# A pair of up projections: both sums of one matrix ahead of the other's, and the second raw sum placed behind a split

## The chip, the cores and the metric

The kernel runs on one core of one Trainium2 chip. The metric is the device time of one execution in microseconds (us). Each kernel is run several times, and the median is what is compared.

## The reference

The program is a trunk of two layers (`DEPTH = 2`) over 512 rows of width 1024, all in float32. Each layer has two half steps with a SwiGLU of inner width 2816, one ahead of a mixer of three head groups and one behind it:

```python
def swiglu(x, w1, w3, w2):
    return (jax.nn.silu(x @ w1) * (x @ w3)) @ w2

for l in range(DEPTH):
    h = x + 0.5 * swiglu(rms_norm(x, ffn1_norm[l]), ffn1_w1[l], ffn1_w3[l], ffn1_w2[l])
    ...
    h = h + y @ w_out[l]
    h = h + 0.5 * swiglu(rms_norm(h, ffn2_norm[l]), ffn2_w1[l], ffn2_w3[l], ffn2_w2[l])
    x = rms_norm(h, final_norm[l])
```

The change touches only `x @ w1` and `x @ w3`, the up projections, of the four half steps. `y` is the mixer's output: a causal convolution, sliding window attention and attention to 256 memory tokens, side by side.

## The kernel before

**Operands in two parts.** A float32 operand is split into a high part and a small rest. ScalarE copies it into the high part (`whi`), VectorE subtracts that from the operand and gets the rest (`wlo`); both instructions are in `split` (lines 147 to 149). A product is then high by high, rest by high and high by rest.

**Chunks and pairs.** The 2816 inner columns are 22 chunks of 128. In each half step chunks 0 to 3 are computed plainly (`up`, `gate`), and the others in pairs f, f + 1 by `up_pair` (line 362): f = 4 in a branch of its own (the plain pair, `PLAIN`), and f = 6, 8 ... 20 in the `else` branch. These are 8 pairs in each of 4 half steps, 32 in all, and the change is in that branch only. The down projection (`begin`, line 546) follows by quarters of the inner width, (first chunk, chunks) = (0, 6), (6, 6), (12, 6), (18, 4). Two chunks of the next quarter are computed ahead of each quarter's down projection, so pairs come in groups: f = 4, 6, then 8, 10, 12, then 14, 16, 18, then 20, with a stretch of down projection behind each group.

**Seven products.** For each matrix i (0 is w1, 1 is w3) a pair is a 2 by 2 block product, done with seven half-size products in place of eight, in the manner of Strassen and Winograd. The left operands are sums of blocks of the normed input, M1 to M7. They are made once for each half step by the class `Seven`, on VectorE and ScalarE, partly while the first pairs run. The right operands are sums of blocks of the weights, each 128 x 1024 words, and each of these units is split once (`unit`, line 357). A pair has seven units:

- raw0 and raw1, the weights of the two matrices as loaded (line 105): product 1 and product 2
- sum0 and sum1, made in place over raw0 and raw1 by two adds each (lines 443 and 444, the raw adds): product 6 and product 3
- X0 and X1 (`wsum`), the sum of two chunks, made by a load that SP issues (line 369) and a second one that GpSimd's queue adds on top (line 370): product 7 and product 5
- z, one half of the next chunk for both matrices (line 374): product 4, for each matrix

The units came in the order raw0, raw1, sum0, sum1, X0, X1, z: three loops over i and a last unit. The first raw add of a matrix reads X of the same matrix, so it has to wait for X to land.

**Products in PSUM.** Products 1, 6 and 5 of a matrix accumulate into one bank `x[i]` (tag `pt`) by `product`, 12 matmuls of 256 columns on line 381. Each time ScalarE copies the running sum to `part` before the next product goes on (lines 438, 449 and 458). Products 2, 3, 7 and 4 go into banks of their own (`po`, `cf`, `mm`) by `beside`, four matmuls of 512 columns and four of 256 on line 389. VectorE adds the pieces up (`add`, lines 399 and 400, and `summed`, line 402) into `u` and `g`. Behind these come `silu` (line 467), the multiplication and the split of the gated result (lines 468 to 472), which the down projection reads.

**Buffers.** There are 3 buffers for the raw tiles (raw0, raw1, z and the weights of the down projection take turns), 3 for `wsum`, and 4 each for `whi` and `wlo`. A load can start when the last reader of what the buffer held is done, which for a weight tile is VectorE's subtract or a raw add. SP issues its loads one after the other, and so does GpSimd.

**The order.** The order on each engine is set by a scheduler, which takes the source as its starting point and places instructions when a model has them ready. `tc.issue_after(x)` makes it place the enclosed instructions behind x only; `queued()` uses it to keep matmuls behind the last ones. While the mixer's weights and the memory tokens are prepared (`memory`, line 678) in the first layer, small instructions of that work lie between those of the pairs: `rsq` (line 195), a power on GpSimd, is one of them.

Of the kernel before, what the change touches and what calls it, by code (L numbers as in the profile page):

```python
# [65 lines left out]
def trunk(ctx: ExitStack, tc: tile.TileContext, xT, memT, pos, w1a, w3a, w2a, w1b, w3b, w2b,  # L66
          wconv, wqk, wvm, wmem, wout, gains, small, rows, consts, out):
    nc = tc.nc
    V, G, A, T = nc.vector, nc.gpsimd, nc.scalar, nc.tensor
# [21 lines left out]
    def bank(shape, tag):  # L91

        if tag == "mm":
            return ps_mm.tile(shape, F32, tag=tag, name=tag)
        return ps_ax.tile(shape, F32, tag=tag, name=tag, bufs=1 if tag == "cf" else 2)

    def tm(name, tag="t", bufs=None):
        return tmp.tile([P, S], F32, tag=tag, name=name, **({"bufs": bufs} if bufs else {}))
# [4 lines left out]
    def raw_tile(src, cols):  # L103
        raw = wst.tile([P, UNIT], F32, tag="raw", name="raw", bufs=3)
        nc.sync.dma_start(raw[:, 0:cols], src)
        return raw
# [40 lines left out]
    def split(hi, lo, x, on):  # L147
        a = A.activation(hi, x, AF.Copy)  # L148
        return a, on.tensor_tensor(out=lo, in0=x, in1=hi.bitcast(F32), op=ALU.subtract)  # L149
# [12 lines left out]
    def pair():  # L162
        return (wst.tile([P, UNIT], F32R, tag="whi", name="whi"), wst.tile([P, UNIT], F32R, tag="wlo", name="wlo"))
# [23 lines left out]
    def blk(k, n=P):  # L187
        return slice(k * n, (k + 1) * n)
# [97 lines left out]
    QW = 512  # L286
# [66 lines left out]
    def gated():  # L353
        p = gated_pair()
        return [at(p, ALL, i, ALL) for i in range(2)]

    def unit(x):
        p = pair()
        split(p[0], p[1], x, V)
        return p  # L360

    def up_pair(l, w13, f, M):

        raw = [raw_tile(w13[i][l, f], D) for i in range(2)]
        X = []
        for i in range(2):

            x = wst.tile([P, UNIT], F32, tag="aux", name="wsum", bufs=3)
            nc.sync.dma_start(x.rearrange("p (f c) -> p f c", f=2), w13[i][l, f : f + 2, :, 0:QW].rearrange("f p c -> p f c"))
            G.dma_start(x, w13[i][l, f + 1], accum_op=ALU.add)  # L370
            X.append(x)
        z = wst.tile([P, UNIT], F32, tag="raw", name="raw", bufs=3)
        for i in range(2):
            nc.sync.dma_start(z[:, blk(i, QW)], w13[i][l, f + 1, :, QW:])
        x0, x1 = blk(0, QT), blk(1, QT)

        def product(ps, w, half, j, first=False):


            for n, (part, q) in enumerate([(0, q) for k in range(4) for q in ((k, 0), (k, 1))] + [(1, (k, 0)) for k in range(4)]):  # L380
                tail[0] = T.matmul(ps, w[part][:, blk(4 * half + q[0])], M.m[j][q[0]][:, q[1]], skip_group_check=True,  # L381
                                   start=first and not n, stop=n == 11)

        def beside(ps, w, half, j, first=False):


            def go(out, part, n):
                for k in range(4):
                    tail[0] = T.matmul(out, w[part][:, blk(4 * half + k)], M.m[j][k][:, 0:n], skip_group_check=True,  # L389
                                       start=first and not part and k == 0, stop=part == 1 and k == 3)  # L390

            go(ps, 0, 2)
            go(ps[:, 0], 1, 1)

        u, g = (tmp.tile([P, 2, S], F32, tag=t, name=t, bufs=n) for t, n in (("u", 1), ("g", 2)))
        part = [tm("part", "sq", 2) for _ in range(2)]
        to = (u, g)

        def add(out, a, b):
            V.tensor_tensor(out=out, in0=a, in1=b, op=ALU.add)  # L400

        def summed(out, ps, a):
            add(out, ps[:, 0], a)
            add(out, out, ps[:, 1])

        if f == PLAIN:
            xy = [bank([P, S], "po") for _ in range(2)]
            zv = [bank([P, S], "pt") for _ in range(2)]
            for i in range(2):
                w = unit(raw[i])  # L410
                product(xy[i][:, x0], w, 0, 1, first=True)
                product(xy[i][:, x1], w, 1, 2)
                A.activation(part[i], xy[i], AF.Copy)
                add(to[i][:, 0, x0], part[i][:, x0], part[i][:, x1])

                add(raw[i][:, 0:QW], raw[i][:, 0:QW], X[i][:, QW:])
                add(raw[i][:, QW:], raw[i][:, QW:], raw[i][:, 0:QW])
            for i in range(2):
                w = unit(raw[i])
                product(xy[i][:, x0], w, 0, 6)  # L420
                A.activation(part[i][:, x1], xy[i][:, x0], AF.Copy)
                product(zv[i][:, x0], w, 1, 3, first=True)
            for i in range(2):
                w = unit(X[i])
                product(xy[i][:, x0], w, 1, 5)
                A.activation(part[i][:, x0], xy[i][:, x0], AF.Copy)
                product(zv[i][:, x1], w, 0, 7)
                add(to[i][:, :, x1], zv[i].rearrange("p (n t) -> p n t", n=2), part[i][:, x0].unsqueeze(1).to_broadcast([P, 2, QT]))
            w = unit(z)
            for i in range(2):  # L430
                product(zv[i][:, x1], w, i, 4)
                add(to[i][:, 1, x0], zv[i][:, x1], part[i][:, x1])
        else:
            x = [bank([P, QT], "pt") for _ in range(2)]
            for i in range(2):
                w = unit(raw[i])
                product(x[i], w, 0, 1, first=True)
                A.activation(part[i][:, x0], x[i], AF.Copy)
                y = bank([P, 2, QT], "po")
                beside(y, w, 1, 2, first=True)  # L440
                summed(to[i][:, 0, x0], y, part[i][:, x0])

                add(raw[i][:, 0:QW], raw[i][:, 0:QW], X[i][:, QW:])
                add(raw[i][:, QW:], raw[i][:, QW:], raw[i][:, 0:QW])
            c, v = [bank([P, 2, QT], t) for t in ("cf", "mm")], []
            for i in range(2):
                w = unit(raw[i])
                product(x[i], w, 0, 6)
                A.activation(part[i][:, x1], x[i], AF.Copy)
                beside(c[i], w, 1, 3, first=True)  # L450
            for i in range(2):
                w = unit(X[i])
                v.append(bank([P, 2, QT], "po"))
                beside(v[i], w, 0, 7, first=True)
                A.activation(to[i][:, 1, x1], v[i][:, 0], AF.Copy)
                add(to[i][:, 1, x1], to[i][:, 1, x1], v[i][:, 1])
                product(x[i], w, 1, 5)
                A.activation(part[i][:, x0], x[i], AF.Copy)
                summed(to[i][:, 0, x1], c[i], part[i][:, x0])
                add(to[i][:, 1, x1], to[i][:, 1, x1], part[i][:, x0])  # L460
            w = unit(z)
            for i in range(2):
                beside(v[i], w, i, 4)
                summed(to[i][:, 1, x0], v[i], part[i][:, x1])
        out = gated()
        for n, sign in enumerate((1.0, -1.0)):
            A.activation(u[:, n], u[:, n], AF.Silu, scale=sign)
        M.gated = V.tensor_tensor(out=g, in0=g, in1=u, op=ALU.mult)
        for n, sign in enumerate((1.0, -1.0)):
            hi, lo = out[n]  # L470
            A.activation(hi, g[:, n], AF.Copy, scale=sign)
            V.scalar_tensor_tensor(out=lo, in0=g[:, n], scalar=sign, in1=hi.bitcast(F32), op0=ALU.mult, op1=ALU.subtract)  # L472
        return out

    def ffn(l, w13, w2, x, sums, factors, last, at_product, aside=None, closing=None):
# [60 lines left out]
        for q, (f0, nf) in enumerate(QUARTERS):  # L536
            ahead = 2 if q + 1 < len(QUARTERS) else 0
            for f in range(f0, f0 + nf + ahead, 2):
                if f not in g:
                    g[f], g[f + 1] = up_pair(l, w13, f, M)  # L540
                    if f == PLAIN:
                        with tc.issue_after(M.gated.ins):
                            rescale = after()
# [614 lines left out]
    for l in range(L):  # L1158
        x, new = nxt.x, Stat("st")
# [163 lines left out]
```

## Time and profile before

| | |
|---|---|
| median of 3 runs | 1759.15 us |
| lowest and highest | 1758.93 and 1760.65 us |
| the profiled execution, its time | 1760.35 us |
| its span in the profile | 1758.5 us |
| TensorE instructions | 10004 |
| bytes moved by DMA | 253.49 MB |

The span runs from the first to the last instruction of the profiled execution; 1.85 us of that execution lie around it. PE is TensorE (PEld its weight loads), DVE is VectorE, ACT ScalarE, POOL GpSimd and SPq the queue that issues most loads. A row of the view in order of time has the start (us from the span's start), the duration, the engine, the line, and output <- inputs; the brackets at its end give the idle time ahead of it and what ended that. A row of the view by stretches has the stretch, its length, and the busy time of each engine in it, with the number of instructions. A row of the DMA table has the queue, the count, the size of each transfer and the median time from issue to landing.

### The profile page before, as it was taken

The page shows a single profiled execution, that of the slowest core. Times are in us where ns is not written, and L with a number is a line of the kernel's source. Part 1 is how long each engine was busy: PE and PEld are TensorE (multiplying, and loading weights), DVE is VectorE, ACT ScalarE, POOL GpSimd, SP SyncE. Part 2 cuts the span into 40 slices and gives each one's busy share as a digit, 9 for nine tenths or more (in the row PEclk, how much of TensorE's full clock was granted, in tenths as well). Part 3 has the DMA queues.
Part 4 walks back from the last instruction along what each step waited for, and adds up shares of the span by engine and source line. Part 5 has one row for each costly group of instructions (what it writes and reads, how often), then busy time and mean ns, then how long its engine had stood idle before and what let it go on. Part 6 is the DMA issues. An engine that isn't in the chain of part 4 may idle for free.

```text
span 1758.5 us, 26405 instructions
## 1 busy us (share of the span) xinstructions
PE 1742.3 (99%) x10004; PEld 1524.0 (87%) x10004; DVE 1370.0 (78%) x2218; ACT 907.7 (52%) x1437; POOL 196.0 (11%) x220
## 2 busy tenths in 40 slices
PE   9999999999999999999999999999999999999997
PEld 7889889888888989898889898988888889898986
DVE  7969878689877868686778787776898768686866
ACT  6546445356765535353656354544567655453533
POOL 1001000006121000000010010000251210000000
PEclk9999999999999999999999999999999999999999
DMA  9456646257247546565566465542671666464632
GB/s 286 112 167 169 179 121 161 73 159 164 86 93 183 142 134 163 143 161 146 150 149 162 150 168 156 158 142 71 162 165 54 136 152 181 131 168 133 153 99 84
DMA packets 96335, 253.49 MB, mean 144 GB/s; under 512 B 9808, under 2 KB 16208, under 8 KB 96208
## 3 DMA queue, kind: packets, MB, share of 16 engines
q1 hardware_dynamic: 77200, 190.45, 34.8%
q0 software_dynamic: 19008, 61.35, 19.5%
q8 instruction: 79, 1.29, 0.3%
q14 instruction: 48, 0.39, 0.1%
HBM read 249.67 MB, written 2.10 MB: 143 GB/s over the span
## 4 chain that ended last, share of the span: by engine, by line
PE 92%; DVE 4%; DMA 2%; issue 1%; ACT 0%; SPq 0%; DVEq 0%; POOLq 0%; ACTq 0%
PE pt L381 16%; PE mm L180 14%; PE mm L182 14%; PE mm L181 14%; PE po L389 13%; PE po L381 2%; PE mm L389 2%; PE cf L389 2%; PE po L180 2%; PE po L182 2%; PE po L181 2%; PE po L928 2%; DMA wsum<-in_w3a 1%; PE mm L876 1%; PE cf L182 1%
## 5 line engine op out<-in xcount | busy, mean ns | idle before, releaser
L148 ACT ACTIVATE whi<-raw 128x1024 fp32r<-128x1024 f32 (+3 forms) x346 | 326.3, 947 | 429.1 <-PE mm L181 202.7
L149 DVE TENSOR_TENSOR wlo<-raw,whi 128x1024 fp32r<-128x1024 f32 (+3 forms) x346 | 374.7, 1088 | 99.4 <-ACT whi L148 98.2
L181 PE MATMUL mm<-glo,whi 128*128 128x512 f32 (+1 forms) x752 | 292.2, 389 | 0.0
L180 PE MATMUL mm<-ghi,whi 128*128 128x512 f32 (+1 forms) x752 | 292.0, 390 | 0.0
L182 PE MATMUL mm<-ghi,wlo 128*128 128x512 f32 (+1 forms) x734 | 285.3, 389 | 0.0
L564 DVE SCALAR_TENSOR_TENSOR h<-mm,h 128x512 f32<-128x512 f32 x126 | 86.3, 688 | 112.2 <-PE mm L182 111.8
L180 PEld LDWEIGHTS mm<-ghi,whi 128*128 128x128 f32 x752 | 141.2, 188 | 29.2 <-DVE h L564 1.2
L181 PEld LDWEIGHTS mm<-glo,whi 128*128 128x128 f32 x752 | 141.3, 188 | 28.4 <-DVE glo L472 0.2
L182 PEld LDWEIGHTS mm<-ghi,wlo 128*128 128x128 f32 x734 | 137.9, 188 | 27.7
L389 PE MATMUL po<-xlo,whi 128*128 128x512 f32 x512 | 139.5, 394 | 0.9 <-DVE g L400 0.9
L1058 DVE SCALAR_TENSOR_TENSOR there<-ypad,par,there 128x512 f32<-128x512 f32 x180 | 136.0, 779 | 1.3
L389 PEld LDWEIGHTS po<-xlo,whi 128*128 128x128 f32 x512 | 89.6, 189 | 15.2 <-DVE g L400 1.8
L180 PE MATMUL mm<-xhi,whi 128*128 128x512 f32 x256 | 101.6, 398 | 0.0
L182 PE MATMUL mm<-xhi,wlo 128*128 128x512 f32 x256 | 99.9, 390 | 0.0
L181 PE MATMUL mm<-xlo,whi 128*128 128x512 f32 x256 | 99.6, 389 | 0.0
L149 DVE TENSOR_TENSOR wlo<-wsum,whi 128x1024 fp32r<-128x1024 f32 x72 | 87.5, 1215 | 0.3 <-ACT whi L148 0.3
L389 PEld LDWEIGHTS po<-xlo,wlo 128*128 128x128 f32 x512 | 78.3, 188 | 10.6
L148 ACT ACTIVATE whi<-wsum 128x1024 fp32r<-128x1024 f32 x72 | 76.2, 1058 | 19.2 <-PE po L389 15.9
L381 PE MATMUL pt<-xhi,whi 128*128 128x256 f32 x576 | 81.9, 283 | 0.0
L389 PE MATMUL po<-xlo,wlo 128*128 128x256 f32 x512 | 81.2, 280 | 0.0
L381 PEld LDWEIGHTS pt<-xhi,whi 128*128 128x128 f32 x576 | 74.8, 190 | 0.5
L381 PE MATMUL pt<-ml,whi 128*128 128x256 f32 x512 | 72.9, 282 | 0.0
(397 smaller groups left out, 3605.7 us busy)
## 6 DMA issues: line engine op xcount, KB each, us to landing
raw<-in_w2a SPq DMA_DIRECT2D x48, 384.0 KB, 3.8
raw<-in_w2b SPq DMA_DIRECT2D x48, 384.0 KB, 3.7
raw<-in_w1a SPq DMA_DIRECT2D x26, 512.0 KB, 3.5
raw<-in_w3a SPq DMA_DIRECT2D x26, 512.0 KB, 3.7
raw<-in_w1b SPq DMA_DIRECT2D x26, 512.0 KB, 3.5
raw<-in_w3b SPq DMA_DIRECT2D x26, 512.0 KB, 3.6
wsum<-in_w1a SPq DMA_DIRECT2D x18, 512.0 KB, 4.5
wsum<-in_w3a SPq DMA_DIRECT2D x18, 512.0 KB, 3.6
```

What stands on the lines that cost most here:

```text
L148: a = A.activation(hi, x, AF.Copy)
L149: return a, on.tensor_tensor(out=lo, in0=x, in1=hi.bitcast(F32), op=ALU.subtract)
L180: T.matmul(ps, a[0], b[0], start=first, stop=False, **more)
L181: T.matmul(ps, a[0], b[1], start=False, stop=False, **more)
L182: tail[0] = T.matmul(ps, a[1], b[0], start=False, stop=last, **more)
L381: tail[0] = T.matmul(ps, w[part][:, blk(4 * half + q[0])], M.m[j][q[0]][:, q[1]], skip_group_check=True, start=first and not n, stop=n == 11)
L389: tail[0] = T.matmul(out, w[part][:, blk(4 * half + k)], M.m[j][k][:, 0:n], skip_group_check=True, start=first and not part and k == 0, st ...
L564: added = V.scalar_tensor_tensor(out=h[:, d, :], in0=ps, scalar=0.5, in1=h[:, d, :], op0=ALU.mult, op1=ALU.add)
L876: tail[0] = T.matmul(pp[i][:, z, :], q, k, start=not masked, stop=True, skip_group_check=True)
L928: tail[0] = T.matmul(po[:, 2 * c + i, :], ptb[:, i, j, :], v, start=(j == 0), stop=(j == nk - 1))
L1058: V.scalar_tensor_tensor(out=cv[:, c, :], in0=ypad[:, c, j : j + S], scalar=conv_w[:, c, j : j + 1], in1=cv[:, c, :], op0=ALU.mult, op1=AL ...
```

## The change

The raw adds leave the first loop and go into the second, each pair of them directly ahead of the split of its sum. The first of the two may only be placed behind the subtract of the unit that was split last (`unit.at`): for matrix 0 that is raw1's, for matrix 1 it is X0's. The second and third loops become one, so the order of the units is now raw0, raw1, sum0, X0, sum1, X1, z. No computation is added or left out.

```diff
     def unit(x):
         p = pair()
-        split(p[0], p[1], x, V)
+        unit.at = split(p[0], p[1], x, V)[1]
         return p
...
                 y = bank([P, 2, QT], "po")
                 beside(y, w, 1, 2, first=True)
                 summed(to[i][:, 0, x0], y, part[i][:, x0])
-
-                add(raw[i][:, 0:QW], raw[i][:, 0:QW], X[i][:, QW:])
-                add(raw[i][:, QW:], raw[i][:, QW:], raw[i][:, 0:QW])
             c, v = [bank([P, 2, QT], t) for t in ("cf", "mm")], []
             for i in range(2):
+                with tc.issue_after(unit.at.ins):
+                    add(raw[i][:, 0:QW], raw[i][:, 0:QW], X[i][:, QW:])
+                add(raw[i][:, QW:], raw[i][:, QW:], raw[i][:, 0:QW])
                 w = unit(raw[i])
                 product(x[i], w, 0, 6)
                 A.activation(part[i][:, x1], x[i], AF.Copy)
                 beside(c[i], w, 1, 3, first=True)
-            for i in range(2):
                 w = unit(X[i])
                 v.append(bank([P, 2, QT], "po"))
                 beside(v[i], w, 0, 7, first=True)
```

Three places show how the programs differ. The first is VectorE in a steady pair, f = 16 of the first half step. `raw_2531` and `raw_2533` are raw0 and raw1 (later sum0 and sum1), `wsum_2535` and `wsum_2538` are X0 and X1, and L149 is the subtract of a split. Before:

```order
L149 TENSOR_TENSOR wlo_2551<-raw_2531,whi_2550 128x1024
L400 TENSOR_TENSOR u_2318<-u_2318,po_2440 128x256
L400 TENSOR_TENSOR raw_2531<-raw_2531,wsum_2535 128x512
L400 TENSOR_TENSOR raw_2531<-raw_2531 128x512
L149 TENSOR_TENSOR wlo_2581<-raw_2533,whi_2580 128x1024
L400 TENSOR_TENSOR u_2318<-cf_2384,part_2320 128x256
L400 TENSOR_TENSOR u_2318<-u_2318,part_2320 128x256
L400 TENSOR_TENSOR g_2319<-g_2319,po_2471 128x256
L400 TENSOR_TENSOR raw_2533<-raw_2533,wsum_2538 128x512
L400 TENSOR_TENSOR u_2318<-u_2318,cf_2384 128x256
L149 TENSOR_TENSOR wlo_2613<-raw_2531,whi_2612 128x1024
```

In the changed program the same stretch begins with raw1's split:

```order
L149 TENSOR_TENSOR wlo_2579<-raw_2533,whi_2578 128x1024
L400 TENSOR_TENSOR raw_2531<-raw_2531,wsum_2535 128x512
L400 TENSOR_TENSOR g_2319<-g_2319,po_2471 128x256
L400 TENSOR_TENSOR raw_2531<-raw_2531 128x512
L400 TENSOR_TENSOR u_2318<-po_2413,part_2320 128x256
L400 TENSOR_TENSOR g_2319<-mm_2381,part_2321 128x256
L400 TENSOR_TENSOR g_2319<-g_2319,part_2321 128x256
L400 TENSOR_TENSOR u_2318<-u_2318,po_2413 128x256
L400 TENSOR_TENSOR g_2319<-g_2319,mm_2381 128x256
L149 TENSOR_TENSOR wlo_2611<-raw_2531,whi_2610 128x1024
L400 TENSOR_TENSOR g_2319<-po_2471,part_2321 128x256
L149 TENSOR_TENSOR wlo_2636<-wsum_2535,whi_2635 128x1024
```

The raw adds of matrix 0 moved from ahead of raw1's split to behind it. Those of matrix 1, which stood ahead of sum0's split, are gone from this stretch and stand behind X0's split, its last row.

The second place is the two queues that load X1 (`wsum_1652`) for f = 10 of the first half step, which is a pair during whose time the memory tokens are prepared. This is the difference on SP's queue:

```order
 L105 DMA raw_1645<-in_w1a 128x1024
+L369 DMA wsum_1652<-in_w3a 128x2x512
 L105 DMA raw_1647<-in_w3a 128x1024
-L369 DMA wsum_1652<-in_w3a 128x2x512
 L369 DMA wsum_1875<-in_w1a 128x2x512
```

And this is the difference on GpSimd's queue, where `rsq` is of `memory`:

```order
 L197 TENSOR_TENSOR rsq4_1395<-hv4_1392,nhalf_113 128x4
+L370 DMA wsum_1652<-in_w3a 128x1024
 L197 TENSOR_TENSOR rsq4_1411<-hv4_1408,nhalf_113 128x4
-L370 DMA wsum_1652<-in_w3a 128x1024
 L370 DMA wsum_1875<-in_w1a 128x1024
```

X1's load moved ahead of raw1's load (`raw_1647`), and its accumulate ahead of the second `rsq`.

The third place is TensorE in the pair f = 6 of the first half step. `pt_782` and `pt_783` are `x[0]` and `x[1]`; `mh`, `ml`, `xhi` and `xlo` hold M1 to M7, and x8 counts equal rows. On `pt_782` the rows that read `mh` are product 1, those that read `ml` product 6, those that read `xhi` product 5. Before:

```order
L381 MATMUL pt_782<-mh_344,whi_784 128x256 x8
L381 MATMUL pt_782<-mh_344,wlo_785 128x256 x4
L381 MATMUL pt_783<-mh_344,whi_814 128x256 x8
L381 MATMUL pt_783<-mh_344,wlo_815 128x256 x4
L389 MATMUL mm_845<-xhi_501,whi_871 128x512 x4
L381 MATMUL pt_782<-ml_345,whi_846 128x256 x8
L381 MATMUL pt_782<-ml_345,wlo_847 128x256 x4
L389 MATMUL mm_845<-xhi_501,wlo_872 128x256 x4
L381 MATMUL pt_783<-ml_345,whi_871 128x256 x8
L381 MATMUL pt_783<-ml_345,wlo_872 128x256 x4
L381 MATMUL pt_782<-xhi_501,whi_896 128x256 x8
L381 MATMUL pt_782<-xhi_501,wlo_897 128x256 x4
```

In the changed program:

```order
L381 MATMUL pt_782<-mh_344,whi_784 128x256 x8
L381 MATMUL pt_782<-mh_344,wlo_785 128x256 x4
L381 MATMUL pt_783<-mh_344,whi_812 128x256 x8
L381 MATMUL pt_783<-mh_344,wlo_813 128x256 x4
L381 MATMUL pt_782<-ml_345,whi_844 128x256 x8
L381 MATMUL pt_782<-ml_345,wlo_845 128x256 x4
L381 MATMUL pt_782<-xhi_501,whi_869 128x256 x8
L381 MATMUL pt_782<-xhi_501,wlo_870 128x256 x4
L389 MATMUL po_873<-xlo_502,whi_869 128x512 x4
L389 MATMUL po_873<-xlo_502,wlo_870 128x256 x4
L381 MATMUL pt_783<-ml_345,whi_902 128x256 x8
L389 MATMUL mm_841<-xhi_501,whi_902 128x512 x4
```

Product 5 of matrix 0 now follows product 6 of the same matrix directly, in the same bank; product 6 and the half of product 3 of matrix 1 that stood between them moved behind it.

## Prediction

> **What bounds the kernel.** I read the page first: the span, the engines' shares, the chain that ended last.
>
> ```profile
> span 1758.5 us, 26405 instructions
> PE 1742.3 (99%) x10004; PEld 1524.0 (87%) x10004; DVE 1370.0 (78%) x2218; ACT 907.7 (52%) x1437; POOL 196.0 (11%) x220
> PE 92%; DVE 4%; DMA 2%; issue 1%; ACT 0%; SPq 0%; DVEq 0%; POOLq 0%; ACTq 0%
> ```
>
> TensorE has work on record for all but 16.2 us of the span, and 92% of the chain is its own. An order of the same matmuls can only win back its idle time, so the next view asks how much of that lies in the up pairs: busy time by stretch. The first five stretches are the only ones around changed pairs in which the record shows TensorE idle; the other three stand for the rest.
>
> ```profile
> core 0: us, PE busy (x) PEld busy (x) DVE busy (x) ACT busy (x) POOL busy (x), PEclk, DMA share, GB/s
> 54.00:100.00 46.00, 44.79 (x319) 41.58 (x318) 40.88 (x60) 27.16 (x41) 3.45 (x4) 1.00 0.64 163
> 134.00:205.00 71.00, 70.32 (x454) 63.59 (x454) 65.27 (x144) 40.62 (x67) 9.62 (x9) 1.00 0.69 179
> 786.00:812.00 26.00, 25.45 (x149) 22.23 (x148) 21.48 (x37) 12.79 (x22) 1.72 (x2) 1.00 0.72 190
> 932.00:970.00 38.00, 37.45 (x266) 34.82 (x265) 31.33 (x47) 20.31 (x32) 3.45 (x4) 1.00 0.73 188
> 1009.00:1072.00 63.00, 62.10 (x419) 56.76 (x418) 54.41 (x93) 37.95 (x63) 7.67 (x8) 1.00 0.63 170
> 576.00:616.00 40.00, 40.00 (x302) 38.46 (x301) 35.00 (x49) 24.76 (x38) 3.45 (x4) 1.00 0.60 159
> 1446.00:1484.00 38.00, 38.00 (x290) 36.63 (x289) 34.75 (x48) 23.94 (x36) 3.47 (x4) 1.00 0.59 155
> 650.00:790.00 140.00, 140.00 (x882) 126.83 (x881) 106.50 (x166) 68.80 (x106) 8.66 (x10) 1.00 0.59 157
> ```
>
> Idle: 1.21, 0.68, 0.55, 0.55 and 0.90 us, together 3.89; elsewhere zero. A matmul's record outlasts its issue, so this is a little short. Rows of TensorE in order of time show by how much.
>
> ```profile
> 182.21 0.63 PE L389 MATMUL po<-xlo,wlo 128*128 128x256 f32 x4
> 183.47 1.19 PE L389 MATMUL cf<-xhi,whi 128*128 128x512 f32 x4 [0.63 <-ACT whi L148]
> 240.58 1.12 PE L381 MATMUL pt<-ml,whi 128*128 128x256 f32 x8
> 241.54 0.64 PE L381 MATMUL pt<-ml,wlo 128*128 128x256 f32 x4
> 242.02 1.09 PE L389 MATMUL cf<-xhi,whi 128*128 128x512 f32 x4
> 242.95 0.63 PE L389 MATMUL cf<-xhi,wlo 128*128 128x256 f32 x4
> 243.42 1.12 PE L381 MATMUL pt<-ml,whi 128*128 128x256 f32 x8
> ```
>
> By the starts, a `product` holds TensorE 1.44 us (240.58 to 242.02) and a `beside` 1.40 (to 243.42); four narrow matmuls take 0.47 (242.95 to 243.42). So the four at 182.21 were issued by 182.68, and the gap behind them cost 0.79 us where the record shows 0.63. Scaled by 0.79/0.63 the idle 3.89 is about **4.9 us, all that the order of the pairs can win**.
>
> **What the change moves.** It adds no instruction, matmul or byte; 2 adds and 2 splits per pair change places, in 32 pairs. The prices, from VectorE, ScalarE and the queues in order of time:
>
> ```profile
> 264.04 0.38 SPq L369 DMA_DIRECT2D wsum<-in_w3a  x1
> 268.16 0.86 POOL L370 DMA_DIRECT2D wsum<-in_w3a  x1 [20.27 <-DVE wlo L149]
> 275.48 0.69 DVE L400 TENSOR_TENSOR raw<-raw,wsum 128x512 f32<-128x512 f32 x1 [2.61 <-DMA wsum<-in_w3a]
> 276.09 0.41 DVE L400 TENSOR_TENSOR g<-mm,part 128x256 f32<-128x256 f32 x1
> 277.08 1.22 DVE L149 TENSOR_TENSOR wlo<-raw,whi 128x1024 fp32r<-128x1024 f32 x1
> 278.22 0.68 DVE L400 TENSOR_TENSOR raw<-raw 128x512 f32<-128x512 f32 x1
> ```
>
> By starts again: a raw add 0.61 us (275.48 to 276.09), a split 1.14 (277.08 to 278.22).
>
> *X1's sum comes earlier and is asked for later.* X1's buffer is the one that X0 of the pair before gives back. In this pair its load was issued at 264.04, the accumulate at 268.16, and VectorE stood 2.61 us for it at 275.48, with sum0's split of the same pair behind that add. Afterwards X0's split lies ahead of sum1's, so the buffer is free one split sooner, SP issues X1 ahead of raw1, and the add waits behind three more splits. I expect this wait to go. It wins nothing by itself: the last of the stretches above (650 to 790), which holds such pairs, has TensorE at 140.00 of 140. It is reserve.
>
> *Fewer adds ahead of raw1 and sum0* (second stretch and fifth). Here VectorE binds: 65.27 of 71 us. The gap at 183.47 waits for sum0. Before, its split had up to four raw adds of its pair ahead, now two: 2 x 0.61 = 1.2 us sooner, more than the 0.79 lost there. Both stretches lose 1.25 x (0.68 + 0.90) = 2.0 us. I take **-1.5**, not all of it, because of the next part; ends -2.0 and 0.
>
> *POOL, in the second stretch only.* The accumulate for X1 now stands ahead of the second `rsq` of `memory`, whose result VectorE multiplies in ahead of X1's split.
>
> ```profile
> 144.63 1.15 POOL L197 TENSOR_TENSOR rsq<-hv,nhalf 128x4 f32<-128x4 f32 x1 [8.61 <-DVE hv L643]
> 147.09 2.52 POOL L197 TENSOR_TENSOR rsq<-hv,nhalf 128x4 f32<-128x4 f32 x1 [1.31 <-DVE ypad L603]
> 169.21 0.38 SPq L369 DMA_DIRECT2D wsum<-in_w3a  x1
> 174.20 0.86 POOL L370 DMA_DIRECT2D wsum<-in_w3a  x1 [17.55 <-DMA wsum<-in_w3a]
> 149.20 1.21 DVE L149 TENSOR_TENSOR wlo<-wsum,whi 128x1024 fp32r<-128x1024 f32 x1
> 152.83 0.65 PE L381 MATMUL pt<-xhi,wlo 128*128 128x256 f32 x4
> ```
>
> From X0's split the path is load to accumulate (4.1 us at 264.04, 5.0 at 169.21), 0.9 for the issue, 1.15 to 2.52 for `rsq`: 6.2 to 8.4. VectorE has some 5.7 us of other work there by the order (a split, two raw adds, 3.3 us of small ones), so it would stand 0.5 to 2.7 us. X1's split was 2.4 us ahead of TensorE (150.41 to 152.83) and everything in front is up to 1.2 sooner, so I price it **0**, ends 0 and +1.5 (2.7 less 1.2). The Trainium skill, SBUF — State Buffer, section "SBUF: two separate sides", says that a GpSimd instruction is shut out of a shared port while VectorE works on two SBUF inputs, which are what the raw adds are. By that rule `rsq` takes the 2.52 and this term is its upper end; the two rows 1.15 and 2.52 agree with it, but nothing here isolates it.
>
> *The first pair behind the plain one* (first stretch and fourth; 1.25 x (1.21 + 0.55) = 2.2 us lost). raw1's split again comes sooner, but TensorE then reaches the last product of the plain pair, which needs M4, and M4's split keeps its place among Seven's sums. I take **-0.5**, nearer to nothing; ends -2.2 and 0. The third stretch loses 0.7 us behind one late add of a pair; I take **-0.3**, ends -0.7 and 0.
>
> *A new wait: product 6, copy, product 5.* Both go into `x[i]`, and the copy on ScalarE has to read the bank in between. Before, at least 1.4 us of other matmuls lay there by the order. Now the pair f = 6 of the first, second and fourth half step has product 5 directly behind product 6.
>
> ```profile
> 242.22 0.39 ACT L449 ACTIVATE part<-pt 128x256 f32<-128x256 f32 x1 [0.79 <-PE pt L381]
> ```
>
> That product's issue ended at 242.02, the copy at 242.61: 0.6 us, three times **+1.8**. Below, 0: TensorE would have stood there anyway. Above, +5.0: a copy of a weight tile ahead of it (1.06, as below) each time. Elsewhere one pair has 0.2 us of matmuls left between (f = 8 of the first half step), one 0.9, all others 1.9 to 5.6, which covers 0.6.
>
> **Sum.** -1.5 + 0 - 0.5 - 0.3 + 1.8 = -0.5 us. The profiled execution took 1760.35 us (span 1758.5 and 1.85 around it), which would become 1759.85; the median of the runs shown is 1.2 lower, so the forecast is 1759.15 - 0.5, about **1758.6**. Ends: -4.9 and +6.5.
>
> **Rivals.**
>
> *Slower: raw1 lands late.* Its buffer returns with sum1's split, which now stands behind X0's split and an add, and SP issues it behind X1.
>
> ```profile
> 258.61 0.33 SPq L105 DMA_DIRECT2D raw<-in_w3a  x1
> 268.62 1.06 ACT L148 ACTIVATE whi<-raw 128x1024 fp32r<-128x1024 f32 x1 [0.51 <-PE pt L381]
> raw<-in_w3a SPq DMA_DIRECT2D x26, 512.0 KB, 3.7
> ```
>
> Load issued 258.61, first read 268.62: 10.0 us, of which 3.7 is the median landing. Later by a split, an add and an issue (1.14 + 0.61 + 0.38), 7.9 remain. It decides once a load takes longer: ScalarE's queue stops, and the part copies behind it too. The accumulate above took 7.3 (268.16 to 275.48), so it is not absurd. Third pairs of a quarter are the thinnest; there are eight. At about 1 us each: +8, 1767. I give it, with the upper end of the copies, 0.17.
>
> *Faster: the starved stretches close and the copies hide.* All of -4.9: 1754.3. For it: VectorE's 2.61 us of waiting turn into reserve just where it binds. Against: M4 and the three copies. 0.13.
>
> *Faster: TensorE is not full at all.* In the last stretch its weight loads are busy 126.83 of 140 us. If a tenth of the open 13.2 came back over 36 pairs of 7 x 2.84 us (716 us), that is 6.7 us: 1752.4. Against: 1.44 and 1.40 us for a product and a beside hold wherever no wait is shown, and the change alters no shape. The Trainium skill, Perfetto Trace Analysis, section "Identifying the Most-Contended Engine", says that busy matmul time is a poor measure of what is left and weight-load time a good one; by that rule this would be the case. I give this rival 0.03.
>
> **How the numbers follow.** A measurement here tells about 0.2%, 3.5 us, from no change: faster is below 1755.6, slower above 1762.7. The forecast and all between these has 0.67, faster 0.13 + 0.03, slower 0.17. The range of 8 in 10 is 1754.5 to 1764.5: the ends of the sum are 1754.3 and 1765.7, and about a tenth is left out on each side, which is most of the two larger rivals.
>
> **What would show it.** Right: no wait of a raw add for X1's sum in steady pairs; TensorE idle in the second and fifth stretch well under 0.7 and 0.9 us; three new waits of TensorE on `part` L449 of about 0.5 at the f = 6 pairs. Wrong: VectorE standing on `rsq` for over 2.5 us near 151 us and TensorE after it; ScalarE waiting for `raw<-in_w3a`; more or less than 1.44 us per product; a total outside the range.

## The result, and the profile after

The changed kernel takes 1775.55 us (median of 4 runs, 1774.80 to 1779.11) beside 1759.04 us for the kernel before in the same comparison: 1.0096 times as long, 95% interval 1.0079 to 1.0114. That is 16.5 us slower, outside the range on record. Its profiled execution took 1779.11 us, 3.6 more than the median; readings of it explain that execution, and the experiments are compared by their medians.

The page of the changed kernel, with the same three rows as before:

```profile
span 1777.3 us, 26372 instructions
PE 1750.1 (98%) x10004; PEld 1527.2 (86%) x10004; DVE 1364.1 (77%) x2218; ACT 904.6 (51%) x1437; POOL 199.1 (11%) x220
PE 86%; DVE 7%; DMA 2%; ACT 2%; issue 2%; POOL 0%; SPq 0%; DVEq 0%; ACTq 0%
```

TensorE is idle for 27.2 us of the record (1777.3 less 1750.1), and was for 16.2. It is also 7.8 us longer busy with the same 10004 instructions, which the last section comes back to. In the chain VectorE went from 4% to 7% and ScalarE from 0% to 2%.

Busy time by stretch, each of the first six a group of changed pairs with the start of the down projection behind it, the last one a steady group:

```profile
core 0: us, PE busy (x) PEld busy (x) DVE busy (x) ACT busy (x) POOL busy (x), PEclk, DMA share, GB/s
54.00:104.00 50.00, 47.43 (x332) 43.71 (x331) 41.91 (x63) 28.42 (x43) 3.46 (x4) 1.00 0.62 163
137.00:215.00 78.00, 73.38 (x458) 65.50 (x457) 66.63 (x142) 41.31 (x71) 11.54 (x9) 0.98 0.61 166
577.00:634.00 57.00, 55.91 (x373) 51.11 (x372) 45.69 (x67) 29.56 (x45) 3.46 (x4) 1.00 0.55 143
925.00:984.00 59.00, 57.53 (x383) 52.56 (x381) 50.40 (x74) 32.53 (x49) 3.46 (x4) 1.00 0.53 139
1007.00:1093.00 86.00, 83.16 (x508) 74.80 (x507) 69.34 (x117) 46.36 (x75) 8.24 (x8) 0.98 0.62 169
1443.00:1510.00 67.00, 65.74 (x416) 59.28 (x415) 54.41 (x79) 34.38 (x52) 4.34 (x5) 1.00 0.55 141
232.00:307.00 75.00, 74.85 (x476) 67.85 (x475) 57.71 (x93) 37.33 (x59) 4.33 (x5) 1.00 0.55 144
```

The idle time is in the first group of all four half steps (2.57, 1.09, 1.47 and 1.26 us) and in the second group of the first and the third (4.62 and 2.84). The steady group has 0.15. The first group of the second half step had none before (48.00 of 48 us busy from 577 to 625).

A record outlasts its issue, so for a fuller count I summed over all matmuls the time from one start to the next, less what that shape usually takes (0.227 us for 512 columns, 0.120 for 256). By this count the changed kernel lost 19.2 us more than before: the first groups 1.5, 1.9, 1.3 and 2.0, the second groups of half steps 1 and 3 6.2 and 3.1, all other groups 1.5 together, and 1.7 outside the pairs. The profiled executions differ by 18.8 us.

What TensorE waited for, from the view of waits (total, times, longest):

```profile
PE mm L180 <- ACT whi L148: 4.8, 4, 2.4
PE pt L381 <- ACT part L449: 4.0, 4, 2.6
PE mm L512 <- ACT whi L148: 1.6, 1, 1.6
PE pt L381 <- DVE xlo L149: 1.5, 2, 0.7
PE po L389 <- DVE u L400: 1.2, 7, 0.3
PE pt L381 <- ACT whi L148: 1.2, 1, 1.2
```

The first row is the down projection waiting for its second weight tile, four times (at 94.24, 204.74, 624.75 and 1501.26). The second is product 5 waiting for the copy of product 6: three short waits and one of 2.6 us. L512 is the start of the program and was there before. Two of these waits show what stands behind them.

**The wait of 2.6 us**, in the second group of the third half step, in order of time. The pair f = 8 begins at 1021.85, the pair f = 10 at 1038.31:

```profile
1021.85 1.11 PE L381 MATMUL pt<-mh,whi 128*128 128x256 f32 x8
...
1027.43 1.21 DVE L149 TENSOR_TENSOR wlo<-wsum,whi 128x1024 fp32r<-128x1024 f32 x1
...
1028.90 0.68 DVE L400 TENSOR_TENSOR raw<-raw,wsum 128x512 f32<-128x512 f32 x1
...
1030.84 0.68 DVE L400 TENSOR_TENSOR raw<-raw 128x512 f32<-128x512 f32 x1
...
1031.73 1.05 ACT L148 ACTIVATE whi<-raw 128x1024 fp32r<-128x1024 f32 x1
1032.81 1.23 DVE L149 TENSOR_TENSOR wlo<-raw,whi 128x1024 fp32r<-128x1024 f32 x1 [0.64 <-ACT whi L148]
1033.45 0.91 POOL L370 DMA_DIRECT2D wsum<-in_w3a  x1 [5.41 <-DMA wsum<-in_w3a]
1034.06 0.33 SPq L105 DMA_DIRECT2D raw<-in_w3a  x1
1038.31 1.12 PE L381 MATMUL pt<-mh,whi 128*128 128x256 f32 x8
1041.14 1.06 ACT L148 ACTIVATE whi<-raw 128x1024 fp32r<-128x1024 f32 x1 [4.98 <-DMA raw<-in_w3a]
1042.11 0.37 ACT L449 ACTIVATE part<-pt 128x256 f32<-128x256 f32 x1
1042.52 2.08 PE L381 MATMUL pt<-xhi,whi 128*128 128x256 f32 x8 [2.62 <-ACT part L449]
```

X0's subtract runs at 1027.43. Behind it come, one after the other, the two raw adds of matrix 1 with small adds between them, ScalarE's copy of sum1, and sum1's subtract at 1032.81. Only then is the raw buffer free, and SP issues raw1 of the next pair at 1034.06, 12.2 us behind the first product of f = 8. ScalarE stands 4.98 us on that load, and the copy of product 6 of the pair f = 8, whose input was long there, stands behind it in ScalarE's queue. The same buffer before:

```profile
1015.64 1.22 DVE L149 TENSOR_TENSOR wlo<-raw,whi 128x1024 fp32r<-128x1024 f32 x1
1016.88 0.33 SPq L105 DMA_DIRECT2D raw<-in_w3a  x1
```

There the pair f = 8 began at 1009.79 (the start of its first matmul on record), so the load was issued 7.1 us behind it: the change made it 5.1 us later.

**A wait for a down projection weight**, with a copy wait ahead of it, in the first group of the second half step:

```profile
615.23 0.64 PE L381 MATMUL pt<-ml,wlo 128*128 128x256 f32 x4
615.90 0.38 ACT L449 ACTIVATE part<-pt 128x256 f32<-128x256 f32 x1 [0.99 <-PE pt L381]
616.34 1.21 PE L381 MATMUL pt<-xhi,whi 128*128 128x256 f32 x8 [0.47 <-ACT part L449]
...
617.27 1.22 DVE L149 TENSOR_TENSOR wlo<-raw,whi 128x1024 fp32r<-128x1024 f32 x1 [0.30 <-ACT whi L148]
617.40 0.86 POOL L370 DMA_DIRECT2D wsum<-in_w3b  x1 [16.06 <-DVE g L400]
618.52 0.33 SPq L105 DMA_DIRECT2D raw<-in_w2b  x1
623.85 0.84 ACT L148 ACTIVATE whi<-raw 128x768 fp32r<-128x768 f32 x1 [3.44 <-DMA raw<-in_w2b]
624.75 0.50 PE L180 MATMUL mm<-ghi,whi 128*128 128x512 f32 x1 [0.62 <-ACT whi L148]
```

The copy of product 6 costs 0.47 us of idle record at 616.34 (0.63 by starts), as in the f = 6 pairs of the first and the fourth half step. The second weight tile is issued at 618.52, at the end of sum1's subtract. ScalarE copies it as soon as it has landed, 5.3 us later, and TensorE takes it up 6.2 us after the issue, having stood 0.62 us for it.

**The late loads also took longer.** In both places GpSimd's accumulate for X1 was issued shortly ahead of the load (0.6 us at 1033.45, 1.1 us at 617.40), and the accumulate was still under way when the load ran. By the landing times in the traces, raw1's load at 1034.06 took 7.0 us (3.7 before, at 1016.88), and the weight tile's at 618.52 took 5.2. The same holds for all four weight tiles of the first row of waits: issued 0.9 to 1.3 us behind such an accumulate, they took 5.2 to 5.7 us. In the kernel before, the second weight tiles of the same four groups were issued with no such accumulate under way and took 3.0 to 3.2. At a landing of 3.7 us raw1 would have been there at 1037.8; ScalarE's copy of it (1.0 us by starts) and that of product 6 (0.4) would then have ended at about 1039.2, ahead of 1039.7, when TensorE came to product 5. So by this estimate TensorE would not have waited there. The delay brings the loads to where the accumulate runs; no run separates the two effects.

### The profile page after: what moved, and what is told of

Read it like the earlier page. It is cut to its first block, busy times and chain, and to the rows that moved or that the text cites. A ratio compares the mean times of both kernels' runs of the same rounds, so it can differ in the third digit from the quotient of the medians.

```text
span 1777.3 us, 26372 instructions
## 1 busy us (share of the span) xinstructions
PE 1750.1 (98%) x10004; PEld 1527.2 (86%) x10004; DVE 1364.1 (77%) x2218; ACT 904.6 (51%) x1437; POOL 199.1 (11%) x220
## 4 chain that ended last, share of the span: by engine, by line
PE 86%; DVE 7%; DMA 2%; ACT 2%; issue 2%; POOL 0%; SPq 0%; DVEq 0%; ACTq 0%
PE pt L381 14%; PE mm L180 14%; PE mm L182 13%; PE mm L181 13%; PE po L389 12%; PE po L381 2%; PE mm L389 2%; PE po L180 2%; PE po L182 2%; PE po L181 2%; PE cf L389 2%; DVE wlo L149 2%; PE po L927 2%; ACT whi L148 1%; PE mm L875 1%
## 5 line engine op out<-in xcount | busy, mean ns | idle before, releaser
L149 DVE TENSOR_TENSOR wlo<-raw,whi 128x1024 fp32r<-128x1024 f32 (+3 forms) x346 | 376.3, 1090 | 124.2 <-ACT whi L148 119.9
L149 DVE TENSOR_TENSOR wlo<-wsum,whi 128x1024 fp32r<-128x1024 f32 x72 | 87.8, 1219 | 3.4 <-ACT whi L148 3.4
```

## The experiments

The chain in these rows has two parts that the change brought: the merged loops (sum1 behind X0 in the source) and the tie by `issue_after`. The first four runs ask whether the raw buffer is the cause, and which part. For each kernel I also took, for the same 32 raw1 loads of the changed pairs, the time from SP's issue to ScalarE's copy that reads the tile (median); it is in the table as "lead". It shows a tendency only: what decides is the few places where the lead runs out. (In the steady third pairs, f = 12 and 18, it is 6.2 us with the change and 5.8 without ties, and neither kernel waits for a load there.)

The kernel before took 1759.3 to 1759.5 us in these comparisons.

| kernel | median, us | ratio to before, 95% | lead, us |
|---|---|---|---|
| before | 1759.04 | | 10.3 |
| the change | 1775.55 | 1.0079 to 1.0114 | 7.3 |
| the change, fourth raw buffer | 1767.53 | 1.0032 to 1.0057 | 14.4 |
| before, fourth raw buffer | 1758.72 | 0.9989 to 1.0006 | 14.4 |
| loops merged, raw adds in the first loop | 1758.26 | 0.9984 to 1.0001 | 8.8 |
| raw adds moved and tied, loops apart | 1760.22 | 0.9995 to 1.0013 | 10.3 |
| the change without ties | 1758.07 | 0.9982 to 1.0000 | 8.8 |
| tie of matrix 0 only | 1762.98 | 1.0011 to 1.0029 | 8.8 |
| tie of matrix 1 only | 1771.68 | 1.0058 to 1.0083 | 7.6 |
| matrix 1 tied to sum0 | 1761.41 | 1.0005 to 1.0023 | 8.8 |
| raw1's and the down projection's splits behind the copy | 1768.10 | 1.0033 to 1.0058 | 7.3 |
| no ties at f = 6 | 1768.30 | 1.0040 to 1.0065 | 7.3 |
| no ties at f = 6, fourth buffer | 1763.24 | 1.0014 to 1.0031 | 14.4 |
| no ties, fourth buffer | 1759.85 | 0.9996 to 1.0014 | 14.1 |

**A fourth raw buffer**, in the changed kernel and in the one before:

```diff
-        raw = wst.tile([P, UNIT], F32, tag="raw", name="raw", bufs=3)
+        raw = wst.tile([P, UNIT], F32, tag="raw", name="raw", bufs=4)
```

(The same number in the two other places. Some tiles of the prologue and the mixer were laid into space that is free at their time to make room; what is computed is the same.)

> The changed kernel with a fourth raw buffer (room for it made by laying four small tiles elsewhere; the output is unchanged). Theory 1: the loss of 16.5 us comes from the raw buffers, since the split of sum1 that gives one back now stands behind that of X0, so that raw1 of the next pair and the second weight tile of the down projection are issued late, ScalarE stands on the load and the copy of product 6 stands behind it. With a fourth buffer these waits go and only the three copies of f = 6 (3 x 0.63 = 1.9 us) and what VectorE lacks are left: 1759 to 1763. Rival (the units' order itself or the place of the raw adds starves TensorE whatever the buffers): 1772 to 1776, as the changed kernel.

> The kernel before with the same fourth raw buffer, as the control. Theory 1: its TensorE waits for a raw load almost nowhere, so 1757.5 to 1760, within 0.1% of the kernel before. If the fourth buffer alone is worth much (under 1755), the gain of the run with the changed kernel says less about the change.

The control stayed at 1758.72, as expected. The changed kernel went to 1767.53: 8.0 us of 16.5 came back, less than theory 1 wanted, and the rival is out as well. The view of waits of the changed kernel with four buffers (its lines are one higher):

```profile
PE pt L382 <- ACT part L450: 1.7, 4, 0.5
PE pt L382 <- DVE xlo L150: 1.5, 2, 0.7
PE mm L513 <- ACT whi L149: 1.2, 1, 1.2
PE po L390 <- DVE u L401: 1.1, 7, 0.2
```

The waits of the down projection for its weights are gone, and the longest wait for a copy is 0.5 us. What stays are the three copies at f = 6, M4, and seven small waits for a bank. So about half of the loss is the return of the raw buffer, and half is something that the buffer does not mend.

**Each part alone**:

```diff
                 beside(c[i], w, 1, 3, first=True)
-            for i in range(2):
                 w = unit(X[i])
```

> The kernel before with the second and third loop made one (units raw0, raw1, sum0, X0, sum1, X1, z), the raw adds left in the first loop. Theory 1: sum1's split still stands behind X0's, so the raw buffer comes back late and most of the loss is there: 1766 to 1776. Rival (the raw adds, tied behind a split, cost the time): 1758 to 1761.

```diff
                 beside(c[i], w, 1, 3, first=True)
+            for i in range(2):
                 w = unit(X[i])
```

(The first is an edit of the kernel before, the second of the changed kernel.)

> The changed kernel with its second loop taken apart again (units raw0, raw1, sum0, sum1, X0, X1, z), the raw adds moved and tied as in the change. Theory 1: sum1's split is ahead of X0's, the buffer comes back nearly as before: 1758 to 1763. Rival (the moved adds cost the time): 1770 to 1776.

Merged loops alone: 1758.26, no loss. Moved and tied adds alone: 1760.22, no difference that can be told. Neither of these halves costs the time; both together do. With the loops apart, though, the tie of matrix 1 is one to sum0's split, the last one ahead of it in the source, and not to X0's; so taking the loops apart also shortens the tie. A kernel further on separates the two. Theory 1 falls where it says that sum1 behind X0 is enough.

**Theory 2: the tie within the merged loops.** The next kernels leave the change as it is and take away the tie of both matrices or of one, and one puts the splits that can wait for a load behind the copy.

```diff
-                with tc.issue_after(unit.at.ins):
-                    add(raw[i][:, 0:QW], raw[i][:, 0:QW], X[i][:, QW:])
+                add(raw[i][:, 0:QW], raw[i][:, 0:QW], X[i][:, QW:])
```

> The changed kernel without issue_after: raw adds in the second loop, order of the units as in the change, but the scheduler may place the first add when it likes. Theory 2 (the loss needs both the merged loops and the tie, because only together they push sum1's add and split, and with it the return of a raw buffer, far enough back): 1757.5 to 1760, like the merged loops alone. Rival (the adds' place in the source, after the first loop, makes the loss): 1770 to 1776.

```diff
-                with tc.issue_after(unit.at.ins):
+                with tc.issue_after(unit.at.ins) if i == 0 else nullcontext():
```

> The changed kernel with the tie for matrix 0 only (its first raw add behind raw1's split; matrix 1 free). Theory 2: sum1's split is not held behind X0's, raw1 of the next pair is read 8.5 us or more after its issue (median), 1758 to 1763. Rival (each tie costs about half): 1765 to 1769.

With `i == 1` in place of `i == 0`:

> The changed kernel with the tie for matrix 1 only (its first raw add behind X0's split; matrix 0 free). Theory 2: this is the tie that sends the buffer back late: median from issue to read of raw1 near 7.3 us, most of the loss, 1769 to 1777. Rival (each tie costs about half): 1765 to 1769.

Without ties 1758.07; with the tie of matrix 0 only 1762.98; with that of matrix 1 only 1771.68. Each is within what theory 2 gave, and the rival's even shares are out: the tie behind X0's split alone costs most of the time. But theory 2 gave no reason for matrix 0's tie to cost anything, and it costs 4.9 us more than no tie. The two longest rows of the view of waits with matrix 1's tie alone:

```profile
PE mm L180 <- ACT whi L148: 6.3, 4, 2.5
PE pt L381 <- ACT part L449: 4.2, 6, 1.3
```

They are the same two kinds of wait as in the changed kernel, but mostly in other places. By the count of lost time (from the first product of f = 6 to that of f = 8), this kernel loses 12.2 us more than before in the four first groups, where the changed kernel loses 6.0, and 0.5 us in the second groups of half steps 1 and 3, where the changed kernel loses 9.4. So the loss in the second groups needs both ties, and the two shares don't simply add up. Of matrix 0's tie one part can be named: every kernel with that tie at f = 6 has waits of 1.5 us for `xlo` (M4), and every kernel without it 0.4 or less. By the same count this tie alone also costs 2.7 us more than no tie in the second groups of half steps 1 and 3.

```diff
-                w = unit(raw[i])
+                with tc.issue_after(copied[0].ins) if i and copied[0] else nullcontext():
+                    w = unit(raw[i])
...
-                w = weights(w2[l, d, :, f0 * P : (f0 + nf) * P], nf * P, V)
+                with tc.issue_after(copied[0].ins):
+                    w = weights(w2[l, d, :, f0 * P : (f0 + nf) * P], nf * P, V)
```

(`copied[0]` is the copy of product 6, set at its line.)

> The changed kernel with raw1's split, and those of the down projection's weights, placed behind the copy of product 6 of matrix 1 of the pair before. The loads are as late as in the changed kernel, but no copy can stand behind a split that waits for them. If the copy behind the late split is the main price: under 1768. If TensorE mostly lacks the late weights themselves: 1771 to 1776.

It took 1768.10, between the two answers, so this one doesn't decide. The lead of raw1 is not better (a wait of 1.2 us for sum0's split stays), and all waits of over 2 us are gone; but the edit also changed when the down projection's first tiles are split and so the order of TensorE's matmuls, and the two effects can't be told apart in it.

**Where, and how long the chain is.** The ties were left out in the pairs f = 6 only, with three and with four buffers; matrix 1's tie was put one unit earlier; and the version that looked best was combined with the fourth buffer.

```diff
-                with tc.issue_after(unit.at.ins):
+                with tc.issue_after(unit.at.ins) if f > 6 else nullcontext():
```

> The changed kernel with the ties left out in the pairs f = 6 only (four pairs of 32). If the losses are local to the pair that has the tie, the first group of each half step no longer loses its 1.5, 1.9, 1.3 and 2.0 us of idle TensorE (6.7 in all) and the rest stays: 1767 to 1770. If the delay is carried along from pair to pair, or the loss moves to f = 8: 1773 to 1776.

> The changed kernel with a fourth raw buffer and no ties in the pairs f = 6. With the fourth buffer alone the first groups still lost 1.3, 0.9, 1.3 and 0.9 us more than the control with four buffers (1758.7): 1767.5 less 4.5, about 1763 (1762 to 1764.5), if what the buffer does not mend is mostly the f = 6 pairs (the copies between products 6 and 5, and late M4). If it is spread over all pairs: 1766 to 1768.

1768.30 and 1763.24, both as expected: the loss at f = 6 is local to those four pairs of 32. By the count of lost time the first groups of the three-buffer kernel lose nothing more than before, and its second groups 6.4 and 3.1, as in the changed kernel. By the medians the four pairs cost 7.3 us with three buffers (roughly, since the five runs lie between 1765.31 and 1771.96) and 4.3 with four, and the two remedies together take back 12.3 of 16.5 us (1775.55 to 1763.24).

```diff
                 beside(c[i], w, 1, 3, first=True)
+                sum0 = unit.at
                 w = unit(X[i])
...
-                with tc.issue_after(unit.at.ins):
+                with tc.issue_after((sum0 if i else unit.at).ins):
```

> The changed kernel with matrix 1's first raw add tied behind sum0's split in place of X0's, one unit earlier. Theory 3 (behind X0's split come two adds, ScalarE's copy and the subtract one after the other before the raw buffer is free, so the length of that chain sets the loss): a chain shorter by one unit, median from issue to read of raw1 8 us or more, 1759 to 1765. Rival (any tie of matrix 1 in the merged loop costs the same): 1769 to 1777.

1761.41, and a lead of 8.8 us, both as theory 3 gave: a tie to the split of one unit earlier takes away 14.1 of the 16.5 us. With this tie and the loops apart it was 1760.22, so with the shorter tie the merged loops cost little. The trace shows where the shorter chain helps: in all four first groups and in the second groups of half steps 1 and 3, the second weight tile is now issued 0.2 to 1.7 us ahead of the accumulate and lands after 3.0 to 3.3 us.

> The candidate for a better kernel: merged loops, raw adds in the second loop, no tie, and a fourth raw buffer. The idle time that is left in the pairs is some 3 us, and the fourth buffer takes away only waits for loads: 1756 to 1758.5. Under 1755.5 would be a gain over the kernel before that can be told; if it is within 0.2% of it, nothing here beats the kernel before clearly.

1759.85, slower than expected and no different from the kernel before. Nothing tried beats the kernel before clearly: the merged loops without ties are the lowest (1758.07, at most 0.18% faster by the interval).

## Why the prediction was wrong

The rival "raw1 lands late" was the right mechanism: ScalarE's queue stops on a late load, and the copies behind it too. It had 0.17, at +8; the sum that gave the forecast put a late load at nothing. The step that failed is the delay, in the prediction's words "Later by a split, an add and an issue (1.14 + 0.61 + 0.38), 7.9 remain". I counted instructions that stand ahead of sum1's split in VectorE's order. The tie made a chain through two engines: X0's subtract, two adds, ScalarE's copy, sum1's subtract. In the pair at 1021.85 the load comes 5.1 us later than before and not 2.1. In the very pair of the prediction, 6.2 us remain and not 7.9:

```profile
270.09 0.33 SPq L105 DMA_DIRECT2D raw<-in_w3a  x1
276.25 1.06 ACT L148 ACTIVATE whi<-raw 128x1024 fp32r<-128x1024 f32 x1 [1.62 <-PE po L389]
```

The runs show that the chain is what counts: the same order of units without the tie loses nothing, and a tie one unit earlier loses 2.1 us (1761.41 beside 1759.29).

The second half of that step was the landing. The prediction set 7.9 us against a median landing of 3.7, and only said that a longer one would decide. In the steady pair above the load landed after 3.4 us and nothing waited. Where TensorE waited, the loads took 5.2 to 7.0 us, beside X1's accumulate. The prediction had X1's sum coming earlier as pure reserve; it did not ask what the earlier accumulate would run beside.

Three more things in this rival's working were off. It looked at raw1 alone; the second weight tile of the down projection takes the same buffers, and waits in the four places of the first row of waits. It named the third pairs of a quarter as the thinnest, by a steady pair (10.0 us from issue to read); the losses are at f = 6 in all half steps and in the second groups of the first and third, where `memory`'s work lies between (in the second layer too, as the rows of `ypad` near 1030 us show) and the loads have less lead. And the price was taken as the idle time alone, when in the profiled execution the two longest waits also lowered the clock (below).

By the terms of the sum:

- *X1's wait becomes reserve, and wins nothing*: right. VectorE's raw adds waited 16.8 us for `wsum` before, in six waits; in the changed kernel the view of waits has none. What the earlier accumulate cost elsewhere is said above.
- *Fewer adds ahead of raw1 and sum0, -1.5*: the gain is there only without the ties. By the same count of lost time, the second groups of half steps 1 and 3 lose 0.7 and 1.2 us less than before in the changed kernel without ties, 1.9 together. With the ties they lose 9.4 us more than before.
- *POOL, 0, upper end +1.5*: right for what it priced. VectorE stood 0.73 us on the second `rsq`, which is the one behind the accumulate, and TensorE not at all. The first `rsq`, which the term left out, took 3.86 us, and TensorE stood 0.59 us behind it on `memory`'s transposition:

```profile
145.29 3.86 POOL L197 TENSOR_TENSOR rsq<-hv,nhalf 128x4 f32<-128x4 f32 x1 [7.55 <-DVE hv L642]
149.19 0.43 DVE L648 TENSOR_TENSOR ypad<-ypad,rsq 128x256 f32<-128x256 f32 x1 [0.90 <-POOL rsq L197]
151.47 0.44 PE L672 MATMUL mm<-cst,ypad 128*128 128x128 f32 x2 [0.59 <-DVE ypad L704]
155.69 0.43 DVE L648 TENSOR_TENSOR ypad<-ypad,rsq 128x256 f32<-128x256 f32 x1 [0.73 <-POOL rsq L197]
```

- *The first pair behind the plain one, -0.5*: wrong sign. M4 was late, as the text said (1.5 us of waits for `xlo`), but the groups lost 1.5 and 1.3 us more, through the copy, the weight tile and M4 itself.
- *The third stretch, -0.3*: right, -0.4 by the same count.
- *Three copies, +1.8*: right; 0.63 each by starts, 1.9 together, ending at 85.51, 616.34 and 1492.69.
- The rival "TensorE is not full at all" is out: steady groups run as before, and no version gained more than the idle time that was known.

What the fourth buffer and f = 6 leave, some 4 us over the kernel before, is about half the waits for a `po` bank: seven, of 0.31 us each by starts, 2.2 together. The rest was not settled.

## What to carry to other kernels

A tie that holds an instruction behind another one may cost nothing where it stands, but it can put a whole chain over several engines behind that point; work out when the last buffer of that chain comes free, and how far ahead of its next reader its next load is then issued, in the tightest place and not in a steady one. Look also at which transfers the delayed load will run beside, since a median landing time may not hold there. Every load that takes turns in that ring counts, those of the next stage too. And where an in-order engine does both the first read of a load and the copies that free PSUM, a late load costs everything behind it.

## What the runs showed of the hardware

**A wait of 2.4 to 2.6 us costs more than itself.** After both such waits of the changed kernel's profiled execution, TensorE's granted clock is down to half for 3.41 us, and full again behind that. For each of the two, the first row is the 3.41 us ahead of the drop, with most of the wait in it, and the second the drop:

```profile
202.80:206.21 3.41, 1.47 (x10) 1.39 (x11) 1.49 (x3) 1.91 (x4) 0.58 (x1) 1.00 0.99 384
206.21:209.62 3.41, 3.41 (x12) 2.90 (x11) 2.09 (x5) 1.19 (x2) 0.29 (x1) 0.50 0.88 187
1039.07:1042.48 3.41, 0.83 (x7) 0.63 (x6) 0.25 (x1) 1.34 (x3) 0.00 (x0) 1.00 1.02 362
1042.48:1045.89 3.41, 3.37 (x14) 3.27 (x15) 2.85 (x5) 1.18 (x4) 0.87 (x1) 0.50 0.52 83
```

The columns are those of the stretches above; 1.00 and 0.50 are the granted clock. Rows of TensorE show what it is for one matmul of 512 columns: 0.43 us from start to start just behind the first wait, 0.23 some microseconds later.

```profile
207.55 0.63 PE L180 MATMUL mm<-ghi,whi 128*128 128x512 f32 x1
207.98 0.63 PE L181 MATMUL mm<-glo,whi 128*128 128x512 f32 x1
...
211.30 0.39 PE L180 MATMUL mm<-ghi,whi 128*128 128x512 f32 x1
211.53 0.40 PE L181 MATMUL mm<-glo,whi 128*128 128x512 f32 x1
```

By the count of lost time these half-clock stretches cost 1.6 us each on top of the waits' 2.6 and 2.8; half of 3.41 is 1.7. A matmul at the lower clock counts as busy, so they are part of the 7.8 us by which TensorE's busy time grew. The kernel with matrix 1's tie alone has the same behind its wait of 2.5 us at 1495.15 (1.7 us more), and nothing behind one of 1.7 us at 620.59. The Trainium skill, TensorE: Matmul & The Clock Gate, section "Why this matters for your kernels", asks for no idle gaps of over about 3 us; here gaps under that already lowered the clock, and the measurement decides.

Two such stretches are 3.2 us, and the profiled execution is 3.6 us over the median of the runs. The mean clock on record is 0.996 for it and 0.997, 0.998 and 0.997 for the other three; one stretch lowers it by 0.001 (1.7 of 1777 us). So it is likely, by this estimate, that the other runs had one or none of them, and that the clock is only a small part of the 16.5 us.
